# An S5 recurrence step in four vector operations, and the S5 output products in pairs, on one Trainium2 core

## The chip, the cores and the metric

The kernel runs on one core of a Trainium2 chip. The core has five instruction queues that matter here: PE (TensorE, matrix products), DVE (VectorE), ACT (ScalarE), POOL (GpSimd) and SP (SyncE, which only starts transfers). DMA engines move data between main memory and the core. TensorE's weight loads are listed apart from its products, as PEld, because they overlap. The metric is the device time of one execution in microseconds (us); the median of three runs is quoted.

## What is computed

The program is one step of a hybrid trunk of four layers on 384 tokens (128 of a prompt, 256 of a sample) and 1024 channels, all in fp32. Layers 0 and 3 are bidirectional S5 layers, layer 1 is a retention layer, layer 2 a Hyena layer. Each layer normalizes, modulates, mixes, gates and adds. The S5 mixer is what the change touches:

```python
ab_re, ab_im = mag * jnp.cos(lam_im * dt), mag * jnp.sin(lam_im * dt)
...
bu_re = jnp.einsum('blgh,gph->blgp', u, bb_re)
bu_im = jnp.einsum('blgh,gph->blgp', u, bb_im)
...
_, _, h_re, h_im = lax.associative_scan(combine, (a_re, a_im, bu_re, bu_im), axis=1)
y = (jnp.einsum('blgp,ghp->blgh', h_re, c_re.astype(F32))
     - jnp.einsum('blgp,ghp->blgh', h_im, c_im.astype(F32)))
...
y = d_skip.astype(F32) * uf          # then the two directions are added
g = jax.nn.gelu(y)
y = g * jax.nn.sigmoid(g @ w_glu.astype(F32) + b_glu.astype(F32))
```

There are 64 groups of 16 channels. Each group drives a complex diagonal state of 64 numbers, once forward and once backward in time.

## The kernel before

**S5 in chunks.** The 384 tokens are cut into 48 chunks of 8. A chunk's contribution to the state is a product with an expanded table (`use_p`, written P0 to P7 in the plan). The state then steps from chunk to chunk (`recur`, written R0 and R1), and the output of a chunk is a sum of three products: its inputs `U` times a Toeplitz table `Tm` (L880), the forward state times an expanded table `CP` (L881), and the backward state times the other half of `CP` (L882). The 64 groups are 8 blocks `m` of 8 groups. R0 steps the states of blocks 0 to 3 (`X` of half 0), R1 those of blocks 4 to 7.

**The recurrence.** The real and imaginary parts of a state lie 16 partitions apart. One step is five DVE operations on 128x64 elements: a shuffle that swaps the parts (L792), the state times the real table `A[:, 0]` (L793), an addition (L794), the swapped state times the imaginary table `A[:, 1]` (L795), and an addition (L796). Prompt (16 chunks) and sample (32 chunks) are two independent chains, and R0 and R1 are independent too; there are 47 steps for each half and layer.

**The output stage.** The loop at L862 goes over the 8 blocks. Half a block (4 groups) needs one tile of `CP`, 16 of them in all (numbered hb), in 6 buffers. In layer 3 all 16 are loaded from main memory, where they were stored before (`scratch_cpd`, POOL's queue, L867). In layer 0 six of them are loaded (SP's queue) and ten are expanded on the spot: two multiplies on DVE for each half (L628 into `CP`, L629 into a tile `xt` of two buffers), and a DMA from POOL's queue that adds `xt` to `CP` (L631): 20 of each. Blocks 2p and 2p+1 share two PSUM tiles: the even block writes partitions 0 to 63, the odd one 64 to 127. After the odd block the pair is copied out (L889, ACT), transposed (L895) and goes through gelu (L901 to L904, ACT and DVE). `Tm` is transposed by PE (L855) from a loaded `Tt`, three blocks ahead of its use. `tick` after each block issues one background unit; here these are modulation products (L378, L385) for a later layer.

**What sets the order.** A scheduler of the framework sets the order of instructions on each engine when the program is built, from the order written, the buffers and times of its own. Each engine then runs its queue in that order. The plan for layer 3 is `A10 U0 U1 P0 A12 P1 A13 U2 P2 A16 P3 R0 U3 P4 P5 P6 P7 R1`.

**Expansion ahead.** `gen_b1` expands the tables for `use_p` early (`BP`, with a temporary of tag `xt`) and, for six hb of layer 0 and all of layer 3, also `CP`, which it stores (L647). Both expansions take their temporaries from the same ring of three `xt` buffers.

Of the kernel before, what the change touches and what calls it, by code (L numbers as in the profile page):

```python
# [10 lines left out]
F32 = mybir.dt.float32  # L11
# [3 lines left out]
OP = mybir.AluOpType  # L15
# [11 lines left out]
NCH = T // Q  # L27
# [13 lines left out]
CT = 1  # L41
# [2 lines left out]
TO = 2  # L44
BT = 2
BT2 = 0
TMB = 3
CPB = 6
PSG = 3
GK0 = 0  # L50
# [54 lines left out]
def hybrid_trunk(ctx: ExitStack, tc: tile.TileContext, I, O, dbg=None, layers=(0, 1, 2, 3)):  # L105
# [15 lines left out]
    def psm():  # L121
        return pm.tile([128, 512], F32, tag="m", name="psm")
# [414 lines left out]
    def gen_setup(j, pool, fpool, pp, defer=None):  # L537
# [70 lines left out]
        def s_sign():  # L608
            A = A8[j] = cst.tile([128, 2, 128], F32, name=f"A{j}")
            V.tensor_copy(A[:, 0], B1[:, 8])  # L610
            V.tensor_scalar(A[:, 1], BI[:, 8], sgn[:, 0:1], None, op0=OP.mult)
            V.tensor_scalar(FI, FI, sgn[:, 0:1], None, op0=OP.mult)
            V.tensor_scalar(B1, B1, sgn[:, 1:2], None, op0=OP.mult)
            V.tensor_scalar(BI, BI, -1.0, None, op0=OP.mult)
# [9 lines left out]
    def expand(out, rot, T1, T2, x, sl, l0, bufs, eng, add):  # L624
        c1 = T1[:, sl, l0:l0 + 4].rearrange("p e l -> p l e").unsqueeze(3).to_broadcast([128, 4, 8, 16])
        c2 = T2[:, sl, l0:l0 + 4].rearrange("p e l -> p l e").unsqueeze(3).to_broadcast([128, 4, 8, 16])
        t = rot.tile([128, 4, 8, 16], F32, tag="xt", name="xt", bufs=bufs)
        eng.tensor_tensor(out, c1, x[:, 0].unsqueeze(2).to_broadcast([128, 4, 8, 16]), op=OP.mult)  # L628
        eng.tensor_tensor(t, c2, x[:, 1].unsqueeze(2).to_broadcast([128, 4, 8, 16]), op=OP.mult)  # L629
        if add is None:  # L630
            nc.gpsimd.dma_start(out, t, accum_op=OP.add)  # L631
        else:
            add.tensor_tensor(out, out, t, op=OP.add)  # L633

    def expand_c(CP, rot, tb, xc, hb, xb, eng, add):
        for d in range(2):
            expand(CP[:, d], rot, tb["B1"], tb["BI"], xc[:, d], slice(1, 9) if d == 0 else slice(8, 0, -1), d * 64 + hb * 4, xb, eng, add)

    def gen_b1(j, hb, tb, rot, xb=3, nb=1, spill=False):
        if hb % nb == 0:  # L640
            tb["bc"] = rot.tile([128, nb, 2, 2, 2, 4, 16], F32, tag="bc", name="bc", bufs=2)
            (nc.gpsimd if hb > 2 else nc.sync).dma_start(tb["bc"], I["s5bc"][j, hb // 4, :, hb % 4:hb % 4 + nb])
        rb, xc = tb["bc"][:, hb % nb, 0], tb["bc"][:, hb % nb, 1]
        if spill:
            CP = rot.tile([128, 2, 4, 8, 16], F32, tag="CP", name="CP", bufs=1)
            expand_c(CP, rot, tb, xc, hb, xb, V, None)
            getattr(nc, SPQ).dma_start(I["cpd"][hb], CP.rearrange("p d g e c -> p (d g e c)"))  # L647
        S.activation(xc, xc, AF.Copy, scale=tb["sgn"][:, 1:2])
        BPs = []
        for d in range(2):  # L650
            BP = rot.tile([128, 4, 8, 16], F32, tag="BP", name="BP", bufs=max(xb, 2))
            expand(BP, rot, tb["F1"], tb["FI"], rb[:, d], slice(7, None, -1) if d == 0 else slice(0, 8), d * 64 + hb * 4, xb, V, G if j else V)
            BPs.append(BP)
        return BPs, xc
# [43 lines left out]
    def s5(i, j, nxt, begun=lambda: None):  # L698
# [70 lines left out]

        def recur(q):  # L770
            gs = slice(q * XH, (q + 1) * XH)
            A1, A2 = Av[:, 0, :, gs], Av[:, 1, :, gs]
            X, XF = Xs[q], XFs[q]
            Xb = X[:, 0, 0, 0:1]
            V.tensor_copy(XF[:, 0], X[:, 0, CC])
# [67 lines left out]
        Tms = []  # L843

        def toeplitz(m):
            kdm = I["kd"][j * 8 + m]
            Tt = rot.tile([128, 8, 128], F32, tag="Tt", name="Tt")
            for t in range(8):
                src = bass.AP(tensor=kdm.tensor, offset=kdm.offset + (7 - t) * 16, ap=[[1920, 16], [240, 8], [1, 128]])
                nc.sync.dma_start(Tt[16 * t:16 * t + 16], src)  # L850
            Tm = rot.tile([128, 8, 128], F32, tag="Tm", name="Tm", bufs=TMB)
            for r in range(2):
                ps = psm()
                for g in range(4):
                    TE.transpose(ps[:, g * 128:(g + 1) * 128], Tt[:, r * 4 + g, :], ident)  # L855
                S.copy(Tm[:, r * 4:r * 4 + 4, :], ps.rearrange("p (g c) -> p g c", c=128))
            Tms.append(Tm)
        for m in range(TMB):
            toeplitz(m)
        for m in range(8):  # L860
            CP = []
            for r in range(2):  # L862
                c = rot.tile([128, 2, 4, 8, 16], F32, tag="CP", name="CP", bufs=CPB if j == 0 else CP1)
                if j == 0 and 2 * m + r not in SPL:
                    gen_c(j, 2 * m + r, tb, rot, c, 2, V, None)
                else:
                    (CQ if j else nc.sync).dma_start(c.rearrange("p d g e c -> p (d g e c)"), I["cpd"][2 * m + r])  # L867
                CP.append(c)
            Tm = Tms[m]
            hf = m % 2  # L870
            if hf == 0:
                pys = [psm(), psm()]
                Ys = rot.tile([128, 8, 8, 16], F32, tag="Ys", name="Ys", bufs=1)
            for r in range(2):
                for g in range(4):
                    gl = r * 4 + g
                    gg = m * 8 + gl
                    o = pys[r][64 * hf:64 * hf + 64, g * 128:(g + 1) * 128]
                    o48 = pys[r][64 * hf:64 * hf + 48, g * 128:(g + 1) * 128]
# [3 lines left out]
            if m + TMB < 8:  # L883
                toeplitz(m + TMB)
            tick(CT)
            if hf == 0:
                continue
            for r in range(2):
                S.copy(Ys[:, :, r * 4:r * 4 + 4, :], pys[r].rearrange("p (g t i) -> p t g i", g=4, t=8))  # L889
            for hf in range(2):  # L890
                fb = m - 1 + hf
                o = 64 * hf
                pg = psm()
                for t in range(8):
# [682 lines left out]
```

## Time and profile before

| What | Value |
|---|---|
| Runs | 1665.21, 1668.08, 1676.65 us; median 1668.08 us |
| Profiled execution | 1671.79 us, of which 1670.0 us are the span of the profile |
| Granted TensorE clock, mean over the span | 0.946 |
| PE / PEld busy | 1480.2 us (89%) / 1316.1 us (79%) |
| DVE busy | 1254.5 us (75%) |
| ACT busy | 695.5 us (42%) |
| POOL busy | 662.3 us (40%) |

A share is a mean over the whole program. Layer 3's output stage lies at 1528.7 to 1587.4 us of the span; layer 0's ends at about 341 us, and its expansions for it begin at about 222 us. A granted clock of 1.00 is TensorE's upper level (2.4 GHz), 0.50 the lower one (1.2 GHz).

### The profile page before, as it was taken

To read this page: it belongs to the slowest core of one execution; us is meant where nothing else is said; L and a number is where in the kernel's file an instruction comes from. 1 tells how busy PE (TensorE), PEld (TensorE's weight loads), DVE (VectorE), ACT (ScalarE), POOL (GpSimd) and SP (SyncE) were. 2 spreads that over 40 slices of the span, in tenths; PEclk is the share of its full clock that TensorE was granted. 3 is DMA by queue.
4 is the path that set the end of the run, shared out by engine and by line. 5 is a ranking of instruction groups with operands and counts; after the bars stand their busy time and mean duration, and the time that the engine had idled before them with its cause. 6 is when DMAs were issued, how large, how long until landed. Compare 5 with 4: busy or idle time off the path is not lost. (4 is left out here: it accounts for less than half of the span.)

```text
span 1670.0 us, 27794 instructions
## 1 busy us (share of the span) xinstructions
PE 1480.2 (89%) x10370; PEld 1316.1 (79%) x10370; DVE 1254.5 (75%) x3123; ACT 695.5 (42%) x1275; POOL 662.3 (40%) x484
## 2 busy tenths in 40 slices
PE   5777777788789998999979999999999999987996
PEld 3555566577579887889978989989999797776996
DVE  8956996579787777755868988888798864398355
ACT  2535422233333333335355445454454543531343
POOL 2111232215175757551225655655666231231221
PEclk7889898799799999999989999999999999997998
DMA  8588499733655555543333222222322363675431
GB/s 351 171 234 245 130 242 249 213 132 141 219 173 180 185 206 182 190 155 127 126 132 95 93 70 84 99 92 83 98 92 76 134 252 108 198 210 187 114 127 63
DMA packets 107807, 261.41 MB, mean 157 GB/s; under 512 B 28535, under 2 KB 68568, under 8 KB 88088
## 3 DMA queue, kind: packets, MB, share of 16 engines
q1 hardware_dynamic: 80768, 200.12, 36.4%
q0 software_dynamic: 11984, 34.87, 7.6%
q10 hardware_dynamic: 14920, 24.65, 4.1%
q8 instruction: 82, 1.34, 0.3%
q14 instruction: 53, 0.43, 0.1%
HBM read 220.37 MB, written 30.83 MB: 150 GB/s over the span
## 5 line engine op out<-in xcount | busy, mean ns | idle before, releaser
L133 POOL TENSOR_TENSOR wl<-wr,wh 128x1024 fp32r<-128x1024 f32 (+2 forms) x99 | 249.8, 2525 | 309.3 <-ACT wh L161 271.5
L161 ACT CAST wh<-wr 128x1024 fp32r<-128x1024 f32 (+4 forms) x211 | 215.9, 1029 | 293.7 <-PE psd L138 215.0
L138 PE MATMUL psd<-hh,wh 128*128 128x384 f32 x880 | 303.7, 347 | 8.9 <-ACT wh L161 5.0
L138 PE MATMUL psd<-hl,wh 128*128 128x384 f32 x880 | 302.8, 344 | 6.8 <-DVE hl L469 6.3
L138 PE MATMUL psd<-hh,wl 128*128 128x384 f32 x880 | 302.8, 345 | 6.0 <-POOL wl L133 3.5
L148 DVE TENSOR_TENSOR wl<-wr,wh 128x1024 fp32r<-128x1024 f32 (+3 forms) x112 | 146.4, 1309 | 71.4 <-ACT wh L161 70.9
L138 PEld LDWEIGHTS psd<-hh,wh 128*128 128x128 f32 x880 | 167.7, 191 | 20.0 <-ACT wh L161 8.4
L138 PEld LDWEIGHTS psd<-hl,wh 128*128 128x128 f32 x880 | 167.5, 190 | 16.2 <-DVE hl L469 9.1
L138 PEld LDWEIGHTS psd<-hh,wl 128*128 128x128 f32 x880 | 167.1, 190 | 14.6 <-issue 5.9
L138 PE MATMUL psd<-wl,hh 128*128 128x256 f32 x384 | 110.3, 289 | 5.2 <-DVE wl L148 3.8
L138 PE MATMUL psd<-wh,hh 128*128 128x256 f32 x384 | 111.1, 293 | 4.0 <-DVE g L531 2.6
L138 PE MATMUL psd<-wh,hl 128*128 128x256 f32 x384 | 109.1, 286 | 0.0
L378 PE MATMUL psn<-wr,sgc 128*32 128x256 f32 x640 | 58.2, 454 | 49.0 <-DMA wr<-in_mod_w_dram 42.8
L138 PE MATMUL psd<-zb,wh 128*128 128x384 f32 x240 | 80.9, 338 | 0.0
L138 PEld LDWEIGHTS psd<-wl,hh 128*128 128x128 f32 x384 | 74.3, 193 | 6.9 <-DVE wl L148 4.7
L138 PEld LDWEIGHTS psd<-wh,hh 128*128 128x128 f32 x384 | 73.7, 193 | 6.1 <-DVE g L531 3.3
L378 PEld LDWEIGHTS psn<-wr,sgc 128*32 128x32 f32 x640 | 20.1, 122 | 70.6 <-DMA wr<-in_mod_w_dram 44.7
L629 DVE TENSOR_TENSOR xt<-BI,xc 128x512 f32<-128x512 f32 x52 | 45.1, 870 | 40.6 <-POOL CP L633 16.6
L138 PEld LDWEIGHTS psd<-wh,hl 128*128 128x128 f32 x384 | 74.1, 193 | 0.1
L633 POOL TENSOR_TENSOR BP<-BP,xt 128x512 f32<-128x512 f32 x32 | 46.0, 1437 | 65.8 <-DVE xt L629 41.5
L628 DVE TENSOR_TENSOR CP<-B,xc 128x512 f32<-128x512 f32 x52 | 54.3, 1076 | 18.8 <-DMA scratch_cpd_dram<-CP 9.7
L629 DVE TENSOR_TENSOR xt<-FI,bc 128x512 f32<-128x512 f32 x64 | 48.8, 769 | 24.7 <-POOL BP L633 8.9
(388 smaller groups left out, 4015.0 us busy)
## 6 DMA issues: line engine op xcount, KB each, us to landing
wr<-in_mod_w_dram SPq DMA_DIRECT2D x40, 1024.0 KB
wr<-in_hy_w_in_dram SPq DMA_DIRECT2D x32, 1024.0 KB
wr<-in_ret_w_in_dram SPq DMA_DIRECT2D x24, 1024.0 KB
wr<-in_s_w_in_dram SPq DMA_DIRECT2D x16, 1024.0 KB
wm<-in_mod_w_dram SPq DMA_DIRECT2D x8, 1024.0 KB
CP<-xt POOLq DMA_DIRECT2D x32, 256.0 KB, 7.7
Tt<-scratch_kd_dram SPq DMA_DIRECT2D x128, 64.0 KB
wr<-in_s_w_glu_dram SPq DMA_DIRECT2D x8, 1024.0 KB
```

Of the source, the lines that this page charges most:

```text
L133: G.tensor_tensor(out, a, b, op=op)
L138: TE.matmul(out, lhs[a], rhs[b], start=start and i == 0, stop=stop and i == len(combos) - 1)
L148: V.tensor_sub(out, a, b)
L161: S.copy(hi, ap)
L378: TE.matmul(ps[q * 32:(q + 1) * 32, :256], sg[:, kb, 6 - 2 * u:38 - 2 * u], raw[:, kb, :], start=u == 0 and k2 == 0, stop=u == 3 and k2 == 1)
L628: eng.tensor_tensor(out, c1, x[:, 0].unsqueeze(2).to_broadcast([128, 4, 8, 16]), op=OP.mult)
L629: eng.tensor_tensor(t, c2, x[:, 1].unsqueeze(2).to_broadcast([128, 4, 8, 16]), op=OP.mult)
L633: add.tensor_tensor(out, out, t, op=OP.add)
```

## The change

1. A recurrence step is four DVE operations. One multiply of 128x128 takes the state times both tables (`A12`), the shuffle then swaps the parts of the second product, and two additions follow. The sign of `A[:, 1]` is turned accordingly. The temporaries `sw` and `m1` have one buffer each instead of two.
2. The output loop goes over pairs of blocks. For each group of four it issues the product with `Tm` for the even and the odd block, then the two forward ones, then the two backward ones, so that neighbouring products write different PSUM halves. The three products have one line now (L882).
3. `Tm` is kept in halves of 4 groups, 7 buffers of a half instead of 3 of a whole, and is made four blocks ahead. `CP` tiles are asked for in the order 0, 2, 1, 3 | 4, 6, 5, 7 | and so on. The two background units of a pair come after it.
4. In `gen_b1` the expansions that are stored get a tag of their own (`xs`, 2 buffers), those for `BP` one `xt` buffer instead of three; `BP` has three buffers in layer 0 and two in layer 3.

Below, most lines after a changed one move down by one: L880 to L882 become L882, L793/L792/L794/L796 become L793/L794/L795/L796, L378 and L385 become L379 and L386, L895 becomes L894.

```diff
-TMB = 3
+TMB = 4
+TMH = 7
...
-            V.tensor_scalar(A[:, 1], BI[:, 8], sgn[:, 0:1], None, op0=OP.mult)
+            V.tensor_scalar(A[:, 1], BI[:, 8], sgn[:, 1:2], None, op0=OP.mult)
...
-        t = rot.tile([128, 4, 8, 16], F32, tag="xt", name="xt", bufs=bufs)
+        t = rot.tile([128, 4, 8, 16], F32, tag=tag, name="xt", bufs=bufs)
...
-    def gen_b1(j, hb, tb, rot, xb=3, nb=1, spill=False):
+    def gen_b1(j, hb, tb, rot, xb=1, nb=1, spill=False):
...
-            expand_c(CP, rot, tb, xc, hb, xb, V, None)
+            expand_c(CP, rot, tb, xc, hb, 2, V, None, "xs")
...
-            BP = rot.tile([128, 4, 8, 16], F32, tag="BP", name="BP", bufs=max(xb, 2))
+            BP = rot.tile([128, 4, 8, 16], F32, tag="BP", name="BP", bufs=2 if j else 3)
...
-                    sw = tmp.tile([128, 2, XH], F32, tag=f"sw{c0}{q}", name="sw")
-                    m1 = tmp.tile([128, 2, XH], F32, tag=f"m1{c0}{q}", name="m1")
-                    V.stream_shuffle(sw, cur, [(x + 16) % 32 for x in range(32)])
-                    V.tensor_mul(m1, cur, A1)
-                    V.tensor_add(dst, dst, m1)
-                    V.tensor_mul(sw, sw, A2)
+                    sw = tmp.tile([128, 2, XH], F32, tag=f"sw{c0}{q}", name="sw", bufs=1)
+                    m1 = tmp.tile([128, 2, 2, XH], F32, tag=f"m1{c0}{q}", name="m1", bufs=1)
+                    V.tensor_mul(m1, cur.unsqueeze(1).to_broadcast([128, 2, 2, XH]), A12)
+                    V.stream_shuffle(sw, m1[:, 1], [(x + 16) % 32 for x in range(32)])
+                    V.tensor_add(dst, dst, m1[:, 0])
                     V.tensor_add(dst, dst, sw)
...
-            Tm = rot.tile([128, 8, 128], F32, tag="Tm", name="Tm", bufs=TMB)
             for r in range(2):
+                Tm = rot.tile([128, 4, 128], F32, tag="Tm", name="Tm", bufs=TMH)
...
-        for m in range(8):
-            CP = []
-            for r in range(2):
+        for m in range(0, 8, 2):
+            CP = {}
+            for r, mm_ in ((r, m + q) for r in range(2) for q in range(2)):
...
-                    TE.matmul(o, U[:, m, gl * NCH:gl * NCH + 64], Tm[:, gl, :], start=True, stop=False)
-                    TE.matmul(o48, Xs[gg // XH][:, 0, 0:48, gg % XH], CP[r][:, 0, g].rearrange("p a b -> p (a b)"), start=False, stop=False)
-                    TE.matmul(o48, Xs[gg // XH][:, 1, 1:49, gg % XH], CP[r][:, 1, g].rearrange("p a b -> p (a b)"), start=False, stop=True)
...
+                    for k in range(3):
+                        for q in range(2):
+                            gg = (m + q) * 8 + gl
+                            X = Xs[gg // XH]
+                            o = pys[r][64 * q:64 * q + (48 if k else 64), g * 128:(g + 1) * 128]
+                            a, b = ((U[:, m + q, gl * NCH:gl * NCH + 64], Tms[m + q, r][:, g, :]),
+                                    (X[:, 0, 0:48, gg % XH], CP[m + q, r][:, 0, g].rearrange("p a b -> p (a b)")),
+                                    (X[:, 1, 1:49, gg % XH], CP[m + q, r][:, 1, g].rearrange("p a b -> p (a b)")))[k]
+                            TE.matmul(o, a, b, start=k == 0, stop=k == 2)
+            for q in range(2):
+                if m + q + TMB < 8:
+                    toeplitz(m + q + TMB)
+                tick(CT)
```

On PE, at the start of layer 3's output stage, the order before is this (psm is the PSUM tile, X_14480 the state of half 0, U the inputs):

```order
L855 MATMUL psm<-ident,Tt 128x128 x4
L378 MATMUL psn<-wr,sgc 32x256 x24
L881 MATMUL psm<-CP,X_14480 48x128
L882 MATMUL psm<-CP,X_14480 48x128
L880 MATMUL psm<-Tm,U 64x128
L881 MATMUL psm<-CP,X_14480 48x128
L882 MATMUL psm<-CP,X_14480 48x128
L880 MATMUL psm<-Tm,U 64x128
```

At the same place the order of the changed kernel is this; products of the two blocks of a pair now stand next to one another:

```order
L882 MATMUL psm<-Tm,U 64x128
L855 MATMUL psm<-ident,Tt 128x128 x4
L379 MATMUL psn<-wr,sgc 32x256 x8
L882 MATMUL psm<-CP,X_14394 48x128 x4
L882 MATMUL psm<-Tm,U 64x128 x2
L882 MATMUL psm<-CP,X_14394 48x128 x4
L882 MATMUL psm<-Tm,U 64x128 x2
```

Of the 384 output products of both layers, 5 of 364 neighbouring pairs wrote different halves before; now all 367 do.

On DVE, in layer 3, towards the end of R0, three chains run at once (one of X_14480, which is R0, and two of X_14481, which is R1). One round of them before is 15 operations, of which these are the first 11:

```order
L792 STREAM_SHUFFLE sw<-X_14481 128x64
L793 TENSOR_TENSOR m_15528<-X_14481,A_4514 128x64
L792 STREAM_SHUFFLE sw<-X_14480 128x64
L793 TENSOR_TENSOR m_15148<-X_14480,A_4514 128x64
L792 STREAM_SHUFFLE sw<-X_14481 128x64
L793 TENSOR_TENSOR m_15521<-X_14481,A_4514 128x64
L795 TENSOR_TENSOR sw<-sw,A_4514 128x64
L794 TENSOR_TENSOR X_14481<-X_14481,m_15528 128x2x32
L795 TENSOR_TENSOR sw<-sw,A_4514 128x64
L794 TENSOR_TENSOR X_14480<-X_14480,m_15148 128x2x32
L795 TENSOR_TENSOR sw<-sw,A_4514 128x64
```

The round of the changed kernel is 12 operations:

```order
L793 TENSOR_TENSOR m_15053<-X_14394,A_4428 128x128
L793 TENSOR_TENSOR m_15420<-X_14395,A_4428 128x128
L793 TENSOR_TENSOR m_15414<-X_14395,A_4428 128x128
L794 STREAM_SHUFFLE sw<-m_15053 128x64
L795 TENSOR_TENSOR X_14394<-X_14394,m_15053 128x2x32
L794 STREAM_SHUFFLE sw<-m_15420 128x64
L795 TENSOR_TENSOR X_14395<-X_14395,m_15420 128x2x32
L794 STREAM_SHUFFLE sw<-m_15414 128x64
L795 TENSOR_TENSOR X_14395<-X_14395,m_15414 128x2x32
L796 TENSOR_TENSOR X_14394<-X_14394,sw 128x2x32
L796 TENSOR_TENSOR X_14395<-X_14395,sw 128x2x32 x2
```

Before R1 starts, layer 3's DVE queue holds 118 operations of R0 before (23.6 steps) and 103 now (25.75 steps).

On DVE in layer 0, around the last step of R1 (X_201), the queue before ends R1 with 18 of the 20 second multiplies (L629) already ahead of it:

```order
L792 STREAM_SHUFFLE sw<-X_201 128x64
L793 TENSOR_TENSOR m_2566<-X_201,A_399 128x64
L795 TENSOR_TENSOR sw<-sw,A_399 128x64
L794 TENSOR_TENSOR X_201<-X_201,m_2566 128x2x32
L796 TENSOR_TENSOR X_201<-X_201,sw 128x2x32
L629 TENSOR_TENSOR xt<-BI,xc 128x512 x2
L628 TENSOR_TENSOR CP<-B_224,xc 128x512 x2
```

In the changed kernel 13 of them stand ahead of it and 7 behind (L630 is what was L629):

```order
L793 TENSOR_TENSOR m_2473<-X_201,A_399 128x128
L629 TENSOR_TENSOR CP<-B_224,xc 128x512
L794 STREAM_SHUFFLE sw<-m_2473 128x64
L795 TENSOR_TENSOR X_201<-X_201,m_2473 128x2x32
L796 TENSOR_TENSOR X_201<-X_201,sw 128x2x32
L391 TENSOR_TENSOR mod_3027<-psn,vec 128x2x4x2
L395 SCALAR_TENSOR_TENSOR sc_3028<-mod_3027,vec 128x16
L630 TENSOR_TENSOR xt<-BI,xc 128x512 x4
```

Five of the second multiplies, with their transfers, thus moved from ahead of R1's end to behind it.

## Rows read from the trace of the kernel before

**Rows 1.** Busy time in 10 us stretches; the last columns are PE clock, DMA share, GB/s

```profile
1510.00:1520.00 10.00, 6.40 (x61) 5.20 (x59) 10.00 (x83) 0.49 (x1) 0.00 (x0) 1.00 0.75 253
1530.00:1540.00 10.00, 10.00 (x59) 9.36 (x58) 7.71 (x48) 1.07 (x2) 1.10 (x2) 0.59 0.18 56
1540.00:1550.00 10.00, 10.00 (x99) 9.63 (x98) 3.97 (x16) 4.66 (x9) 2.63 (x4) 1.00 0.75 195
...
300.00:310.00 10.00, 1.74 (x7) 1.34 (x8) 6.01 (x15) 1.50 (x3) 3.17 (x4) 0.50 0.76 214
```

**Rows 2.** Chain of waits through layer 3's output stage: start, length, engine, piece

```profile
1528.69 0.67 PE psm L881 x2
1529.36 0.43 PE psm L882 x2
...
1539.16 0.22 PE psm L880 x2
...
1587.42 0.56 PE psd L138 x2
```

**Rows 3.** PE timeline where `use_p` runs: start, length, form, partitions and columns

```profile
1434.05 1.95 PE L746 MATMUL psm<-PB,U 128*64 128x256 f32 x16
1435.93 0.44 PE L138 MATMUL psd<-hh,wh 128*128 128x384 f32 x1
```

**Rows 4.** PE timeline in layer 0, where two blocks' products happen to meet

```profile
331.77 0.27 PE L881 MATMUL psm<-CP,X 128*48 128x128 f32 x1
331.78 0.32 PE L880 MATMUL psm<-Tm,U 128*64 128x128 f32 x1
...
332.16 0.27 PE L881 MATMUL psm<-CP,X 128*48 128x128 f32 x1
332.27 0.38 PE L882 MATMUL psm<-CP,X 128*48 128x128 f32 x2
```

**Rows 5.** DVE timeline in layer 3's recurrence; in brackets what ended idle time

```profile
1472.60 0.18 DVE L775 COPY XF<-X 128x32 f32<-128x32 f32 x1 [0.92 <-ACT X L758]
...
1526.00 0.21 DVE L792 STREAM_SHUFFLE sw<-X 128x64 f32<-128x64 f32 x1
...
1527.35 0.21 DVE L792 STREAM_SHUFFLE sw<-X 128x64 f32<-128x64 f32 x1
...
1529.73 0.23 DVE L792 STREAM_SHUFFLE sw<-X 128x64 f32<-128x64 f32 x1
...
1530.65 0.22 DVE L792 STREAM_SHUFFLE sw<-X 128x64 f32<-128x64 f32 x1
```

**Rows 6.** L793 between R1's start and R0's end: ns min/median/max, first and last start

```profile
L793 DVE TENSOR_TENSOR m<-X,A x58: 201/206/2441, 1473.3 to 1527.8; 128x64 f32<-128x64 f32 x58
```

**Rows 7.** DVE timeline of two 128x128 operations near the program's start

```profile
24.79 0.28 DVE L601 TENSOR_TENSOR B<-B,pa 128x128 f32<-128x128 f32 x1
24.99 0.28 DVE L602 TENSOR_TENSOR BI<-BI,pb 128x128 f32<-128x128 f32 x1
```

**Rows 8.** Layer 0's expansions: the tile CP's accumulating DMAs, and DVE's first and last xt

```profile
L631 POOL DMA_DIRECT2D CP<-xt x20: 839/853/881, 223.3 to 322.2; - x20
...
DMA to landing us min/median/max: 3.3/7.6/11.1
...
222.32 0.68 DVE L629 TENSOR_TENSOR xt<-BI,xc 128x512 f32<-128x512 f32 x1
...
312.24 1.29 DVE L629 TENSOR_TENSOR xt<-BI,xc 128x512 f32<-128x512 f32 x2
```

**Rows 9.** PE timeline and ACT timeline of layer 0: first product of half 1, and the last copy

```profile
312.38 0.61 PE L881 MATMUL psm<-CP,X 128*48 128x128 f32 x2
...
341.48 0.58 ACT L889 COPY Ys<-psm 128x512 f32<-128x512 f32 x1 [6.19 <-PE psm L882]
```

**Rows 10.** DMA issues of layer 3's output stage: count, KB each, median us to landing

```profile
CP<-scratch_cpd_dram POOLq DMA_DIRECT2D x10, 512.0 KB, 4.1
```

**Rows 11.** Waits of DVE in 40 to 166 us: us in total, times, longest

```profile
DVE xt L629 <- DMA CP<-xt: 7.0, 3, 4.6
```

More of the change, by code (lines that the diff above doesn't have):

```diff
@@ L622, in gen_setup, with expand @@
         return dict(B1=B1, BI=BI, F1=F1, FI=FI, sgn=sgn, dsk=dsk, dmask=dmask)
-    def expand(out, rot, T1, T2, x, sl, l0, bufs, eng, add):
+    def expand(out, rot, T1, T2, x, sl, l0, bufs, eng, add, tag="xt"):
         c1 = T1[:, sl, l0:l0 + 4].rearrange("p e l -> p l e").unsqueeze(3).to_broadcast([128, 4, 8, 16])
         c2 = T2[:, sl, l0:l0 + 4].rearrange("p e l -> p l e").unsqueeze(3).to_broadcast([128, 4, 8, 16])
-        t = rot.tile([128, 4, 8, 16], F32, tag="xt", name="xt", bufs=bufs)
+        t = rot.tile([128, 4, 8, 16], F32, tag=tag, name="xt", bufs=bufs)
         eng.tensor_tensor(out, c1, x[:, 0].unsqueeze(2).to_broadcast([128, 4, 8, 16]), op=OP.mult)
@@ L633, in expand, with expand_c @@
             add.tensor_tensor(out, out, t, op=OP.add)
-    def expand_c(CP, rot, tb, xc, hb, xb, eng, add):
+    def expand_c(CP, rot, tb, xc, hb, xb, eng, add, tag="xt"):
         for d in range(2):
-            expand(CP[:, d], rot, tb["B1"], tb["BI"], xc[:, d], slice(1, 9) if d == 0 else slice(8, 0, -1), d * 64 + hb * 4, xb, eng, add)
-    def gen_b1(j, hb, tb, rot, xb=3, nb=1, spill=False):
+            expand(CP[:, d], rot, tb["B1"], tb["BI"], xc[:, d], slice(1, 9) if d == 0 else slice(8, 0, -1), d * 64 + hb * 4, xb, eng, add, tag)
+    def gen_b1(j, hb, tb, rot, xb=1, nb=1, spill=False):
         if hb % nb == 0:
@@ L771, in recur @@
             gs = slice(q * XH, (q + 1) * XH)
-            A1, A2 = Av[:, 0, :, gs], Av[:, 1, :, gs]
+            A12 = Av[:, :, :, gs]
             X, XF = Xs[q], XFs[q]
@@ L842, in s5 @@
         rot = mk(e2, "s5c", 2)
-        Tms = []
+        Tms = {}
         def toeplitz(m):
@@ L855, in toeplitz @@
                     TE.transpose(ps[:, g * 128:(g + 1) * 128], Tt[:, r * 4 + g, :], ident)
-                S.copy(Tm[:, r * 4:r * 4 + 4, :], ps.rearrange("p (g c) -> p g c", c=128))
-            Tms.append(Tm)
+                S.copy(Tm, ps.rearrange("p (g c) -> p g c", c=128))
+                Tms[m, r] = Tm
         for m in range(TMB):
             toeplitz(m)
-        for m in range(8):
-            CP = []
-            for r in range(2):
+        for m in range(0, 8, 2):
+            CP = {}
+            for r, mm_ in ((r, m + q) for r in range(2) for q in range(2)):
                 c = rot.tile([128, 2, 4, 8, 16], F32, tag="CP", name="CP", bufs=CPB if j == 0 else CP1)
-                if j == 0 and 2 * m + r not in SPL:
-                    gen_c(j, 2 * m + r, tb, rot, c, 2, V, None)
-                else:
[L867 to L873, printed above, removed]
+                if j == 0 and 2 * mm_ + r not in SPL:
+                    gen_c(j, 2 * mm_ + r, tb, rot, c, 2, V, None)
+                else:
+                    (CQ if j else nc.sync).dma_start(c.rearrange("p d g e c -> p (d g e c)"), I["cpd"][2 * mm_ + r])
+                CP[mm_, r] = c
+            pys = [psm(), psm()]
+            Ys = rot.tile([128, 8, 8, 16], F32, tag="Ys", name="Ys", bufs=1)
             for r in range(2):
@@ L876, in s5 @@
                     gl = r * 4 + g
-                    gg = m * 8 + gl
-                    o = pys[r][64 * hf:64 * hf + 64, g * 128:(g + 1) * 128]
-                    o48 = pys[r][64 * hf:64 * hf + 48, g * 128:(g + 1) * 128]
-                    TE.matmul(o, U[:, m, gl * NCH:gl * NCH + 64], Tm[:, gl, :], start=True, stop=False)
-                    TE.matmul(o48, Xs[gg // XH][:, 0, 0:48, gg % XH], CP[r][:, 0, g].rearrange("p a b -> p (a b)"), start=False, stop=False)
-                    TE.matmul(o48, Xs[gg // XH][:, 1, 1:49, gg % XH], CP[r][:, 1, g].rearrange("p a b -> p (a b)"), start=False, stop=True)
[L883 to L887, printed above, removed]
+                    for k in range(3):
[11 more added lines that the diff above has]
+                tick(CT)
             for r in range(2):
@@ L890, in s5 @@
             for hf in range(2):
-                fb = m - 1 + hf
+                fb = m + hf
                 o = 64 * hf
```

## The prediction

> **What bounds the kernel now.** I read first the busy time by stretch, to see which engine is full in each stage that the change touches; then the chain of waits, to see what sets the end of a stage; then the timelines, to price single instructions.
>
> In layer 3 two stages follow one another. While the states step, DVE is full and PE is not: 10.00 of 10 us against 6.40 [rows 1]. From 1530 on PE is full, 10.00 of 10, and DVE has 3.97 of 10 [rows 1]. The chain agrees: from 1528.69 to 1587.42 it runs through PE's products, one after another, 0.43 us each at first and 0.22 from 1539 [rows 2]. The reason for the two prices is in the granted clock, 0.59 in 1530 to 1540 and 1.00 after [rows 1], close to the lower and at the upper level (1.2 and 2.4 GHz); PE had been waiting for R0 before that. So in this layer what shortens R0's end counts, and then what shortens PE's 58.7 us.
>
> Layer 0 is another thing. In 300 to 310 PE is busy for 1.74 and DVE for 6.01 of 10 us [rows 1]; neither is full. PE's first product of the second half starts at 312.38, when R1 ends, and the last copy of sums waits until 341.48 for PE [rows 9]. What fills the time is the expansion of the ten `CP` tiles: 20 accumulating DMAs are issued from 223.3 to 322.2, each landing 3.3 to 11.1 us after its issue, and their multiplies are spread from 222.32 to 312.24, 9 pairs of them in 89.9 us, 10.0 us for a pair [rows 8]. R1's steps share the DVE queue with these multiplies, and a multiply that waits for its `xt` buffer holds up all behind it.
>
> **Part 1, the step in four operations.** Operations on 64 elements start 0.1355 us apart when two chains alternate: ten of them lie between 1526.00 and 1527.35 [rows 5], so a step is 5 x 0.1355 = 0.68 us. Operations on 128x128 start 0.20 apart [rows 7]. The new step is 0.20 + 3 x 0.1355 = 0.61, a saving of 0.07. Its bounds are zero, if the wide multiply costs as much as the two it replaces (0.27), and 0.1355, if it costs as little as one of them; the row of two 128x128 operations is the nearest in shape, and I take it. A chain that runs alone waits for itself: 0.92 us a step, from 1529.73 to 1530.65 [rows 5]. There the new step is as long or longer, since the shuffle now waits for the multiply (0.98, estimated as 0.92 plus the 0.07 by which a 128x128 operation starts its successor later). That holds only at ends of chains.
>
> From R1's start at 1472.60, which ACT's copy of the last block gates [rows 5], to R0's end 58 steps are run [rows 6], in an interleaved order: 58 x 0.07 = 4. Before R1 starts, the queue now holds two more steps of R0, done while PE was the slower one, another 1.3. R0 ends 5 us earlier (0 to 9). Some of these multiplies last up to 2.44 us beside the usual 0.2 [rows 6]; I leave that as it is.
>
> The Trainium skill bears on this (VectorE: DVE Perf Modes, "The DRAIN you can't avoid"): an operation there does not start until the pipe of the one before it is empty. By it a step would go from 5 x 0.21 to 0.28 + 3 x 0.21, and the 58 steps would save 8 us. The trace disagrees: the 0.21 us operations start 0.1355 apart [rows 5].
>
> **Part 2, pairs of products in layer 3.** Neighbouring products now write different halves of the partitions. The trace has two places where that happens already. In `use_p` 8 products of 256 columns alternate between the halves and take 1.88 us, 1434.05 to 1435.93, 0.235 each [rows 3]; in one half two times 0.2165 would be due for as many columns, so the ratio is 0.54. In layer 0, where a block of one half happens to run beside one of the other, eight records, which is four products, start between 331.77 and 332.27, 0.125 each [rows 4]. I take 0.12 at the high clock. The bounds are 0.11 (the two fully beside one another) and 0.2165 (no overlap).
>
> The 58.7 us of the stage split as follows. 10.5 us go by at the low clock, 24 products with a group of modulation products. The other 168 products take 168 x 0.2165 = 36.4. What is left, 11.8, is transposes, modulation products and waits. With the change the low clock lasts as long as before, I assume, and in 10.5 us it passes 40 products (0.24 each); 152 remain, 152 x 0.12 = 18.2; the rest is 11.8, and 1 for the second background unit, which now comes at once. Sum 41.5, a gain of 17 (14 to 19).
>
> Two things stand under this cover before and come near the surface after. The `CP` loads, ten of 512 KB with 4.1 us to landing [rows 10], must come in 41 us instead of 59: 5.24 MB were 28.5% of the DMA engines' time and would be 40%. And gelu and the copies of sums on ACT and DVE, 4.66 and 3.97 us in 10 [rows 1], would be 6.6 and 5.6 in 10. Both fit on paper. R1 is no bound: its states are needed by the third pair, half the stage after the start.
>
> **Part 3, layer 0.** The same pairing is worth 96 x 0.1 = 10 us here after R1's end, if products are what the end waits for, and it ends when the last expansion lands. In the new order 13 of the 20 second multiplies stand ahead of R1's last step, where 18 stood; at 10.0 us a pair the 13th comes at 222 + 60 = 282, and R1 ends at about 289, not 312. The expansions go on at their pace: the 20th issue comes at about 318, its landing 7.6 later at 326, and the last products end about 4 us after that. So the end moves from 341 to 330, a gain of 11. If the last landing stays where it was, 322.2 + 7.6 = 330, and eight more for the last pair of blocks, the gain is 3; if fewer stalls of R1 also quicken the multiplies, 16. I take 11, since the order moves five multiplies behind R1.
>
> **Part 4, the temporaries.** With a tag of their own the stored expansions no longer hold up those for `BP`: DVE waited 7.0 us in all for these transfers in the early stage [rows 11]. On the other side `BP` has one `xt` instead of three, so each expansion waits for POOL's or DVE's addition of the one before. Between a gain of 7 and a loss of 3 I take 0, because PE and DMA are both pressed there by the weights. `Tm` in halves and the order of `CP` tiles are counted in parts 2 and 3.
>
> **The sum.** 5 + 17 + 11 = 33. The profiled execution took 1671.8; 1671.8 - 33 = 1638.8. The median of the runs shown is 3.7 lower than that execution, so the forecast is 1635.
>
> **The rivals.** *Layer 0 gives nothing*, because the expansions and their transfers run to the same end whatever PE does. For it speaks that neither PE nor DVE is full there [rows 1]; against it, that R1's end gated PE until 312 [rows 9] and has moved forward in the order. It would give 5 + 17 = 22, so 1646.
>
> *The reload of `CP` takes over in layer 3.* The six buffers come free by pairs of blocks, so that eight loads are wanted in two bursts, on a queue behind POOL's other work. The stage would be about 50 us, midway between 41.5 and 58.7, which loses 8.5 of the gain: 1643, or 1654 if layer 0 gives nothing either. For it speaks the closer supply (40% of the DMA time), against it the 4.1 us to landing [rows 10].
>
> *The pairs do not overlap.* Then part 2 is zero and layer 0 keeps 4 us from R1's earlier end: 5 + 4 = 9, so 1659. The rows on both places speak against it [rows 3, 4]. The Trainium skill (TensorE: Matmul & The Clock Gate, "Part 3: Packing small matmuls — row/col tiling") says that a weight load overlaps products in flight only when their row groups differ, and the two of a pair use the same rows. By that rule the stage would stay at 58.7. The trace bears out the other reading, since in both places the products share all 128 rows as well.
>
> *The low clock stays (slower).* In stretches where PE had gaps the clock was granted at 0.50 [rows 1]. If the shorter products leave PE waiting between pairs, and it stays at 1.2 GHz through the stage, the stage is 10.5 + 2 x (18.2 + 12.8) = 72.5 us, 14 longer than before; with layer 0's gain lost in the same way and the dense products behind both stages begun at the low clock (some 5 us each), the sum is -5 + 14 + 10 = +19: 1687. It costs half of each microsecond that is spent at the low clock beyond the first 10.5, so the kernel is slower than before from about 45 us of it in a stage of 64, layer 0's gain lost. Against it speaks that PE was full through the low stretch, 10.00 of 10, and the clock rose within it [rows 1].
>
> **Chances.** Forecast 0.50; layer 0 gives nothing 0.25; the reload takes over 0.08; no overlap 0.07; the low clock stays 0.04; a larger gain (layer 0 up to 16, early waits gone, R0 earlier by 9) 0.06. A measurement of this kernel can tell a change of about 1% from none, that is 16.7 us: below 1651 is faster, above 1685 slower. Faster takes nearly all of the first two, the larger gain and half of the reload: 0.81. Slower is 0.02 to 0.04, 0.03. The rest, 0.16, is within 1%. The range of 8 in 10 leaves out the cases of no overlap and of the low clock and half of the larger gain: 1619 to 1653.
>
> **What would show it.** In the changed profile the four-operation rounds should start 0.61 us a step apart, and the 128x128 multiply 0.20 before its successor; layer 3's products should run at 0.12 each after some 10 us of low clock, the stage lasting 41 to 43 us between R0's end and the first dense product; in layer 0 R1 should end near 289 and the last copy of sums near 330. The forecast is wrong if in layer 3 PE waits for `CP` or for gelu between the pairs, if the 128x128 multiply costs 0.27, or if PE's last product in layer 0 still waits for a landing at 330 or later.

## The result: 1653.18 us, and where the profile after differs

| | before | changed |
|---|---|---|
| Median of 8 runs each | 1669.07 us | 1653.18 us (1649.24 to 1660.7) |
| Ratio of the changed kernel to that before | | 0.9896, 95% interval [0.9875, 0.9918] |
| Profiled execution / its span | 1671.79 / 1670.0 us | 1654.23 / 1652.1 us |
| Mean granted TensorE clock | 0.946 | 0.942 |

The change makes the kernel 1.0% faster, 17 us by the ratio. The forecast was 1635 us and a gain of 33, so half of it came; 1653.18 lies at the upper end of the range, which is 1653. Two stages of layer 3 carry the account. The product stage, from the first product with R0's states to the first dense product, took 50.5 us where 58.7 stood [rows 2] and 41.5 were forecast. From R1's start to that first product with R0's states it is 50.4 us, 5.7 less than before. In this profile the first dense product comes 18.6 us earlier (1568.8 against 1587.4). The other 4.7 are there when R1 of layer 3 starts (1467.87 against 1472.60 [rows 5]): 3.4 of them already when R0 of layer 0 starts, 1.3 from there on. So 3.4 + 1.3 + 5.7 + 8.2 = 18.6.

Single traces differ in these parts. In the pairs alone and in the run with one ring of xt, which have the same output loop, the stage takes 46.5 and 45.8 us. In two runs whose edits lie in layer 3 alone, R1 of layer 3 starts at 1463.5 and 1477.7. So the 4.7 us ahead of it cannot be put down to the change, and the stage is worth 8 to 13.

**The step.** The DVE timeline of the changed kernel in layer 3, with two chains running and later with one:

```profile
1465.57 0.49 DVE L793 TENSOR_TENSOR m<-X,A 128x128 f32<-128x128 f32 x2
...
1465.98 0.23 DVE L794 STREAM_SHUFFLE sw<-m 128x64 f32<-128x64 f32 x1
1466.11 0.22 DVE L795 TENSOR_TENSOR X<-X,m 128x64 f32<-128x64 f32 x1
...
1466.79 0.49 DVE L793 TENSOR_TENSOR m<-X,A 128x128 f32<-128x128 f32 x2
...
1467.87 0.26 DVE L776 COPY XF<-X 128x32 f32<-128x32 f32 x1
...
1519.38 0.29 DVE L793 TENSOR_TENSOR m<-X,A 128x128 f32<-128x128 f32 x1
...
1520.36 0.29 DVE L793 TENSOR_TENSOR m<-X,A 128x128 f32<-128x128 f32 x1
```

Two steps lie between 1465.57 and 1466.79, 0.61 us a step where 0.68 stood [rows 5]. One chain alone needs 0.98, where it needed 0.92. Both are as forecast. The copy at 1467.87 is R1's start.

**The pairs.** The PE timeline of the changed kernel in layer 3, second pair of blocks:

```profile
1531.09 0.39 PE L882 MATMUL psm<-Tm,U 128*64 128x128 f32 x4
1531.31 0.60 PE L882 MATMUL psm<-CP,X 128*48 128x128 f32 x8
1531.74 0.39 PE L882 MATMUL psm<-Tm,U 128*64 128x128 f32 x4
```

A product is two records, so twelve records are six products. They take 0.65 us, 0.108 each, half of the 0.22 of one half alone [rows 2] and at the lower bound of the forecast. By the Trainium skill (TensorE: Matmul & The Clock Gate, "Part 3: Packing small matmuls — row/col tiling") a weight load overlaps products in flight only when their row groups differ. The trace disagrees: the two products of a pair use the same rows and cost half as much side by side.

**The hole.** Busy time of the changed kernel in layer 3 (columns as in [rows 1]), and below it the chain of waits:

```profile
1510.00:1520.00 10.00, 7.16 (x76) 5.20 (x76) 9.81 (x74) 0.49 (x1) 0.00 (x0) 0.94 0.65 201
...
1530.00:1540.00 10.00, 8.58 (x116) 7.84 (x114) 7.79 (x29) 4.50 (x10) 4.26 (x6) 1.00 1.08 299
1540.00:1550.00 10.00, 2.20 (x10) 1.86 (x11) 0.00 (x0) 1.17 (x2) 0.00 (x0) 0.64 0.80 205
1550.00:1560.00 10.00, 10.00 (x120) 9.48 (x118) 3.89 (x6) 4.45 (x9) 3.07 (x4) 0.68 0.07 14
```

```profile
1518.30 5.84 PE psm L882 x72
...
1528.71 10.38 DMA Tt<-scratch_kd_dram
...
1543.01 6.49 DMA Tt<-scratch_kd_dram
1549.74 1.94 PE psm L855 x8
1551.68 1.48 PE psm L894 x16
1553.16 7.00 PE psm L882 x96
...
1563.37 5.39 PE psm L882 x96
1568.76 0.56 PE psd L139 x2
```

Where PE was full before, it is busy for 2.20 of 10 us in 1540 to 1550. The chain says what it waits for: not for `CP`, not for gelu, but for the tables `Tt` of blocks 6 and 7, which land at 1549. What stands behind that wait in PE's queue is the third pair of blocks, whose own tables were ready. The DMA engines are full while the first of these `Tt` are on their way (share 1.08 in 1530 to 1540, then 0.80). The first 48 products after the hole (96 records) take 7.00 us and the next 48 take 5.39: the granted clock is 0.64 in the hole and 0.68 in the stretch behind it.

The DMA issues of this stage, changed kernel; the `CP` loads land in 9.1 us (median), before in 4.1 [rows 10]:

```profile
CP<-scratch_cpd_dram POOLq DMA_DIRECT2D x10, 512.0 KB, 9.1
```

**Layer 0.** Of the changed kernel, DVE's timeline from R0's start on, PE's, and ACT's last copy:

```profile
161.17 0.18 DVE L776 COPY XF<-X 128x32 f32<-128x32 f32 x1
...
303.67 0.69 DVE L630 TENSOR_TENSOR xt<-BI,xc 128x512 f32<-128x512 f32 x1 [10.84 <-DMA CP<-xt]
...
310.91 0.69 DVE L630 TENSOR_TENSOR xt<-BI,xc 128x512 f32<-128x512 f32 x1 [4.83 <-DMA CP<-xt]
311.51 0.55 DVE L903 SCALAR_TENSOR_TENSOR gf<-gx,psm 128x384 f32<-128x384 f32 x1
```

```profile
312.21 0.70 PE L882 MATMUL psm<-Tm,U 128*64 128x128 f32 x4 [7.34 <-DVE gf L903]
```

```profile
334.05 0.59 ACT L888 COPY Ys<-psm 128x512 f32<-128x512 f32 x1 [7.26 <-PE psm L882]
```

R1 ends at 290.1, and PE's first product of the second half with a state starts at 299.6, 13 us earlier than in [rows 9]. But the last copy comes only 7.4 earlier. R0's start, in the kernel before:

```profile
164.57 0.18 DVE L775 COPY XF<-X 128x32 f32<-128x32 f32 x1 [1.08 <-ACT X L758]
```

So 3.4 of the 7.4 us lie ahead of R0. From R0's start to the last copy it is 172.9 us, before 176.9, and from R0's start to R1 of layer 3 it is 1306.7, before 1308.0. A multiply that waits for its `xt` buffer, that is for an accumulating DMA to land, holds up gelu's L903 behind it on DVE; gelu holds a PSUM tile, and PE waits 7.34 us for it.

### The profile page after: what moved, and what is told of

Read it like the earlier page. It is cut to its first block, busy times and chain, and to the rows that moved or that the text cites. A ratio compares the mean times of both kernels' runs of the same rounds, so it can differ in the third digit from the quotient of the medians.

```text
span 1652.1 us, 27609 instructions
## 1 busy us (share of the span) xinstructions
PE 1460.5 (88%) x10370; PEld 1290.5 (78%) x10370; DVE 1250.0 (76%) x2935; ACT 693.9 (42%) x1275; POOL 663.5 (40%) x484
## 5 line engine op out<-in xcount | busy, mean ns | idle before, releaser
L139 PEld LDWEIGHTS psd<-hh,wh 128*128 128x128 f32 x880 | 168.2, 192 | 26.2 <-issue 14.3
L379 PE MATMUL psn<-wr,sgc 128*32 128x256 f32 x640 | 57.0, 449 | 30.7 <-DMA wr<-in_mod_w_dram 25.5
L630 DVE TENSOR_TENSOR xt<-BI,xc 128x512 f32<-128x512 f32 x52 | 47.2, 911 | 44.9 <-DMA CP<-xt 18.9
L630 DVE TENSOR_TENSOR xt<-FI,bc 128x512 f32<-128x512 f32 x64 | 51.8, 809 | 17.8 <-POOL BP L634 9.8
L632 POOL DMA_DIRECT2D CP<-xt x32 | 28.0, 929 | 92.7 <-DVE xt L630 43.6
L634 POOL TENSOR_TENSOR CP<-CP,xt 128x512 f32<-128x512 f32 x32 | 50.1, 1565 | 31.1 <-DVE xt L630 19.5
```

What stands on the lines that cost most here:

```text
L139: TE.matmul(out, lhs[a], rhs[b], start=start and i == 0, stop=stop and i == len(combos) - 1)
L379: TE.matmul(ps[q * 32:(q + 1) * 32, :256], sg[:, kb, 6 - 2 * u:38 - 2 * u], raw[:, kb, :], start=u == 0 and k2 == 0, stop=u == 3 and k2 == 1)
```

## The experiments

Ratios are to the kernel before. The main theory was that the gain is the sum of the step and the pairs, and that the missing part of layer 3 is the wait for `Tt`. The rivals are named with each run.

**The step alone.** The kernel before with the four-operation step and nothing else:

```diff
-V.stream_shuffle(sw, cur, [(x + 16) % 32 for x in range(32)])
-V.tensor_mul(m1, cur, A1)
-V.tensor_add(dst, dst, m1)
-V.tensor_mul(sw, sw, A2)
+V.tensor_mul(m1, cur.unsqueeze(1).to_broadcast([128, 2, 2, XH]), A12)
+V.stream_shuffle(sw, m1[:, 1], [(x + 16) % 32 for x in range(32)])
+V.tensor_add(dst, dst, m1[:, 0])
 V.tensor_add(dst, dst, sw)
...
```

> The kernel before with the four-operation step alone (products, Tm and expansion buffers as before). Theory (the gain in layer 3 is the sum of an earlier end of R0 and of shorter products): R0 ends some 7 us earlier against the dense products ahead of it, the output stage stays near 58 us, layer 0 changes by less than 4 us; about 1662 us, 7 below the kernel before. Rival (the step is the whole of the gain, and pairing gives nothing): 1653 us, as the whole change.

Measured: 1663.64 us, 0.9961 [0.9942, 0.9979], 6.5 us less. Layer 3's products run from 1522.7 to 1578.9, 56.2 us. From R1's start to the first product with R0's states it is 50.0 us, before 56.1. The rival falls, and the theory holds for layer 3: the step is worth about its own part and no more. It misses in layer 0, where the change was to be under 4 us: the last copy comes at 328.47, 13 us earlier than before (162.6 us from R0's start, before 176.9). Nothing of that is left when R1 of layer 3 starts (1472.7 against 1472.6).

**The pairs alone.** The changed kernel with the old five operations in `recur` (the diff above, the other way).

> The changed kernel with the old five-operation step. Theory: R0 ends as late as before, layer 3's output stage is about 50 us with the same hole before the third pair, layer 0 ends 7 us earlier; about 1658 to 1660 us. Rival (pairing gives nothing): 1669 us. Rival (the step gives nothing): 1653 us.

Measured: 1662.74 us, 0.9939 [0.9916, 0.9961], 10.2 us less. The output stage is 46.5 us long, where 50 were expected, and the hole is in it. That stage (columns as in [rows 1]) and the waits of PE in it:

```profile
1527.40:1573.90 46.50, 37.78 (x481) 35.41 (x481) 23.26 (x95) 17.18 (x34) 11.51 (x16) 0.85 0.56 162
```

```profile
PE psm L856 <- DMA Tt<-scratch_kd_dram: 8.7, 2, 7.0
PE psm L883 <- DVE X L797: 3.4, 1, 3.4
```

The two parts add up: 6.5 + 10.2 = 16.7, the whole change 17.4. Both rivals fall, that of a step worth nothing narrowly: the interval begins at 0.9916, and that of the whole change ends at 0.9918.

**Halves in turn.** The changed kernel with the 24 products of the even block ahead of the 24 of the odd one:

```diff
-for r in range(2):
-    for g in range(4):
-        gl = r * 4 + g
-        for k in range(3):
-            for q in range(2):
+for q in range(2):
+    for r in range(2):
+        for g in range(4):
+            gl = r * 4 + g
+            for k in range(3):
```

> The changed kernel with the products of a pair written one block after the other (24 of the even block, then 24 of the odd one), so that neighbouring products write the same PSUM half; all else as in the change. Theory (neighbours in different halves run beside one another): products start 0.22 us apart instead of 0.11, 5 us more for each of the four pairs of layer 3 where PE is not waiting anyway; layer 3's output stage 58 to 62 us, about 1662 us or more. Rival (the pairs do not overlap; the shorter stage comes from the other order and the earlier tables): 1653 us and 0.11 to be seen nowhere or here too.

Measured: 1668.17 us, 0.9983 [0.9967, 0.9999]. Nearly all of the gain in time is gone. PE's timeline of this run in layer 3:

```profile
1558.03 0.38 PE L882 MATMUL psm<-Tm,U 128*64 128x128 f32 x2
1558.25 0.60 PE L882 MATMUL psm<-CP,X 128*48 128x128 f32 x4
1558.69 0.38 PE L882 MATMUL psm<-Tm,U 128*64 128x128 f32 x2
```

One product (two records) takes 0.22, three take 0.66, so the same instructions in another order take twice as long. The stage is 55.6 us, shorter than the 58 to 62 expected; PE waits for `Tt` only 0.8 us in it. The slower products cover the tables. The step's part is still there in this trace (50.1 us from R1's start to the first product with R0's states); why the time shows less than step and stage together was not taken apart.

**The transposes later.** The changed kernel; the transposes of blocks 6 and 7 are written behind the third pair's products, their loads stay:

```diff
+    return lambda: turn(m, Tt)     # toeplitz: loads now, transposes when called
...
+while late:
+    late.pop(0)()
 for q in range(2):
     if m + q + TMB < 8:
-        toeplitz(m + q + TMB)
+        f = toeplitz(m + q + TMB)
+        if m == 2 and j == 1:
+            late.append(f)
+        else:
+            f()
```

> The changed kernel, but in layer 3 the transposes of the tables of blocks 6 and 7 are written behind the third pair's products instead of ahead of them; their loads stay where they are. Theory (PE stands in its own queue behind transposes whose tables land at 1549 us, while all that the third pair needs is there): the third pair starts at about 1540 instead of 1553, the output stage shrinks from 50 to about 42 us, 1645 us. Rival (the third pair's own CP tiles or states are late, since the DMA engines are full): the hole stays, the wait is put down to CP, 1652 us.

Measured: 1646.79 us, 0.9863 [0.9834, 0.9892], 22.9 us less, 5.5 better than the change, though the two intervals overlap. The stage is 44.6 us. The theory held in direction and not in size: the third pair no longer waits for the tables, and the wait has moved behind it, to the fourth. Waits of PE in that stage:

```profile
PE psm L858 <- DMA Tt<-scratch_kd_dram: 5.4, 1, 5.4
...
PE psm L886 <- DMA CP<-scratch_cpd_dram: 1.4, 1, 1.4
```

**The tables earlier.** The changed kernel with four `Tt` buffers in layer 3, so that the last loads no longer wait for transposes and stand ahead of the GLU's weights in SP's queue:

```diff
-Tt = rot.tile([128, 8, 128], F32, tag="Tt", name="Tt")
+Tt = rot.tile([128, 8, 128], F32, tag="Tt", name="Tt", bufs=4 if j else 2)
```

> The changed kernel with four buffers for the loaded tables Tt in layer 3 instead of two, so that all their loads stand ahead of the weights for the GLU in SP's queue. Theory (the hole is made by the last tables, which are asked for when two Tt buffers come free and then share full DMA engines with 5 MB of CP and 2 MB of weights): no wait for Tt is left, the output stage shrinks from 50 us to 41 to 44, 1645 us, at least as good as the late transposes. Rival (the DMA engines are simply too full, whatever the order; then something else is late, CP or the GLU's weights): 1650 us or more, and the dense products behind the stage wait for their weights.

Measured: 1642.77 us, 0.9835 [0.9798, 0.9872], 27.5 us less, 10 better than the change. Whole stage of the changed kernel, then of this one (columns as in [rows 1]):

```profile
1518.30:1568.80 50.50, 40.15 (x497) 36.97 (x498) 24.15 (x88) 18.73 (x37) 11.50 (x16) 0.83 0.59 176
```

```profile
1514.90:1552.30 37.40, 36.38 (x497) 33.93 (x497) 24.02 (x88) 18.80 (x37) 11.50 (x16) 0.93 0.60 211
```

PE waits 1.0 us for `CP` and not at all for `Tt`; the stage is 37.4 us. The dense products behind it wait 0.9 us for the casts of their weights, so the rival falls: the DMA engines had room for everything, in another order. The granted clock is 0.93 instead of 0.83; with the hole goes a stretch of low clock.

**Half expansions.** Two runs leave out the 20 second multiplies and the 20 accumulating DMAs of layer 0's output stage, so that its ten expanded `CP` tiles hold half a sum: once with pairs and once with the step alone.

```diff
+eng.tensor_tensor(out, c1, x[:, 0].unsqueeze(2).to_broadcast([128, 4, 8, 16]), op=OP.mult)
+if add == "half":
+    return
 t = rot.tile([128, 4, 8, 16], F32, tag=tag, name="xt", bufs=bufs)
-eng.tensor_tensor(out, c1, x[:, 0].unsqueeze(2).to_broadcast([128, 4, 8, 16]), op=OP.mult)
...
-gen_c(j, 2 * mm_ + r, tb, rot, c, 2, V, None)
+gen_c(j, 2 * mm_ + r, tb, rot, c, 2, V, "half")
```

> The changed kernel, but in layer 0's output stage the ten tiles of CP that are expanded on the spot get the first multiply alone: the second multiply and the accumulating DMA are left out (20 of each). Theory (layer 0's end is set by these transfers and by the multiplies that wait for them in DVE's queue): the last copy of sums comes some 25 us earlier than in the changed kernel (near 310 instead of 334), of which a part is given back in layer 1. Rival (R1 and the products set the end): it stays within 5 us.

> The kernel with the four-operation step alone, with the same second multiplies and accumulating DMAs of layer 0's output stage left out. Theory (with the expansions gone, products bound layer 0, and pairing is worth some 10 us there): layer 0's output stage ends 10 us later than in the run with pairs and half expansion. Rival (pairing is worth nothing in layer 0 even then): both end alike.

Measured: 1635.31 us, 0.9781 [0.9745, 0.9816], and 1643.06 us, 0.9841 [0.9805, 0.9877]. The last copy of layer 0, with pairs and then with the step alone:

```profile
297.47 0.58 ACT L890 COPY Ys<-psm 128x512 f32<-128x512 f32 x1 [1.63 <-PE psm L884]
```

```profile
310.29 0.59 ACT L890 COPY Ys<-psm 128x512 f32<-128x512 f32 x1 [0.65 <-PE psm L883]
```

With the expansions the same copy came at 334.05 and 328.47. So multiplies and transfers together do set layer 0's end, by 37 us with pairs and 18 without, and only without them are the pairs worth something there: 12.8 us. Yet when R1 of layer 3 starts, the run with pairs is behind (1451.7 against 1449.8): these 12.8 us are given back on the way. In the run with pairs PE is busy for 3.75 of 10 us in 300 to 310, waiting for the casts of the GLU's weights (3.2 us for ACT, 2.7 for DVE). How the rest is given back was not taken apart.

**One ring of xt again.** The changed kernel with the expansion buffers of before:

```diff
-def gen_b1(j, hb, tb, rot, xb=1, nb=1, spill=False):
+def gen_b1(j, hb, tb, rot, xb=3, nb=1, spill=False):
...
-expand_c(CP, rot, tb, xc, hb, 2, V, None, "xs")
+expand_c(CP, rot, tb, xc, hb, xb, V, None)
...
-BP = rot.tile([128, 4, 8, 16], F32, tag="BP", name="BP", bufs=2 if j else 3)
+BP = rot.tile([128, 4, 8, 16], F32, tag="BP", name="BP", bufs=max(xb, 2))
```

> The changed kernel with one ring of three xt buffers for both kinds of expansion again, and three BP buffers in both layers. Theory (the split gains and costs about as much: it takes away DVE's early waits for the accumulating DMAs, 7 us in all, and makes PE wait for BP at the start of layer 1, where the trace after shows 9.0 us and that before 0.2): 1650 to 1655 us, no wait for BP at 430 to 460. Rival (the split is worth its 7 us): 1659 us.

Measured: 1658.1 us, 0.9908 [0.9879, 0.9937]; the change has 0.9896 [0.9875, 0.9918]. The split is worth nothing that these runs can tell. DVE's early waits of 40 to 166 us, of this run and, below, of the changed kernel:

```profile
DVE xt L630 <- DMA CP<-xt: 9.9, 4, 7.2
```

```profile
DVE xt L630 <- DMA CP<-xt: 2.8, 2, 1.9
```

The split takes most of that wait away (7.0 before [rows 11]), as meant. At the start of layer 1 PE waits for `BP` 9.0 us in the changed kernel, 4.1 here and 0.2 in the kernel before. The expectation that none would be left was wrong: part of that wait comes from elsewhere.

**Three xt buffers.** The run with early tables, and one more `xt` buffer where layer 0 expands on the spot:

```diff
-gen_c(j, 2 * mm_ + r, tb, rot, c, 2, V, None)
+gen_c(j, 2 * mm_ + r, tb, rot, c, 3, V, None)
```

> The run with early tables, and three xt buffers instead of two for the tiles that layer 0 expands in its output stage. Theory (a multiply that waits for its xt buffer, up to 10.8 us in the trace after, holds up gelu behind it on DVE, and PE behind gelu): layer 0's last copy of sums comes 5 to 10 us earlier than with two, half of that is given back in layer 1, 1639 us against 1643. Rival (the transfers themselves are the bound, since the DMA engines are full): the waits turn into waits of PE for the landing, 1643 us.

Measured: 1635.28 us, 0.9783 [0.9753, 0.9814], 36 us less than before, the best version of this study. DVE's wait for `CP<-xt` in layer 0, 18.9 us in the changed kernel and 13.9 with early tables, is down to 1.0; the longest is now the wait for `xc`:

```profile
DVE CP L629 <- DMA xc<-in_s5bc_dram: 10.9, 3, 4.7
...
DVE xt L630 <- DMA CP<-xt: 1.0, 2, 0.8
```

The last copy of layer 0, of this run and, below, with two buffers and early tables:

```profile
324.61 0.59 ACT L888 COPY Ys<-psm 128x512 f32<-128x512 f32 x1 [0.74 <-PE psm L882]
```

```profile
330.47 0.59 ACT L888 COPY Ys<-psm 128x512 f32<-128x512 f32 x1 [7.18 <-PE psm L882]
```

R0 starts at 168.2 and at 162.6, so from there to the last copy it is 156.4 us, against 167.9 with two buffers (167.6 to 173.2 in all full traces with the loop over pairs and two buffers). PE waits 0.6 us for a landing, so the rival (the transfers are the bound) falls; holding up the queue was. In time the gain over early tables, some 8 us, is not clear of the noise: the two intervals overlap.

**Layer 0 block by block.** The run with early tables, with layer 0's old output loop (products, order of `CP`, three tables ahead) and the new one for layer 3 alone:

```diff
+for m in range(0 if j == 0 else 8, 8):
+    ...                                  # the loop of the kernel before
-for m in range(0, 8, 2):
+for m in range(8 if j == 0 else 0, 8, 2):
```

> Layer 3 as in the run with early tables; layer 0's output loop goes block by block again, as before the change (products, order of CP tiles, three tables ahead), with the four-operation step. Theory (with the expansions on the spot a pair needs four CP tiles at once, and that costs layer 0 as much as its shorter products bring: 172.8 us from the start of R0 to the last copy in the trace after, 162.5 in that of the step alone): layer 0 ends some 10 us earlier, and with half of it given back in layer 1 the time is 1638 us. Rival (the difference of the two traces is chance, or is given back wholly): 1643 us or more.

Measured: 1645.47 us, 0.9851 [0.9821, 0.9881], against 0.9835 [0.9798, 0.9872] with pairs in both layers. The theory fell. From R0's start to the last copy it is 166.9 us, with pairs 167.9; the 172.9 of the changed kernel's trace lies within what changes from one trace with pairs to another (167.6 to 173.2). In layer 0 the pairs cost nothing and bring nothing that these runs can tell.

## Why the prediction was half right

The time lies at the upper end of the range, and the mechanism was right in part. By its own chances the prediction gave 0.81 to a time below 1651 and 0.16 to one within 1%; the median of 1653.18 is of the second kind.

1. **The step** (predicted 5 us; measured 5.7 at R0's end, 6.5 in time alone). Right in each term: 0.61 for two chains, 0.98 for one, two more steps of R0 ahead of R1. By the Trainium skill (VectorE: DVE Perf Modes, "The DRAIN you can't avoid") the next operation starts when the pipe is empty, unless it is one that is not held back. The trace shows again that these are not: the 64-element operations of a step start 0.13 apart and last 0.22.

2. **Pairs in layer 3** (predicted 17, between 14 and 19; measured 8.2, in two other traces with the same loop 12.2 and 12.9). The price of a product in a pair was right, 0.108 against 0.12. The step that failed is the sentence that two things come near the surface, `CP` loads and gelu, and that both fit on paper. A third one was not costed: the tables of the last two blocks. They are asked for when `Tt` buffers come free, behind 2 MB of weights on SP's queue, and share the DMA engines with the `CP` loads. Before, the slow products covered that; the halves in turn show the cover, 0.8 us of wait against 8.7 in the pairs alone. Early tables give 37.4 us, better than the 41.5 forecast. So the products were priced soundly, and the loss is this wait with the clock that it takes along. One term was too large: the sum let 40 products go by in 10.5 us at the low clock, but in the changed kernel the first 36 (72 records) take 5.84.

3. **The rival "the reload takes over"** gave 50 us for the stage and a total of 1643 or 1654. Its price was met and its mechanism was not: the DMA engines were crowded, as it said, but what came late were tables, in front of which PE's queue stood. `CP` itself was waited for 0.5 us between the second pair's products. That a time near 1654 came out of it is luck.

4. **Layer 0** (predicted 11; 7.4 at the last copy, 4.0 of it behind R0's start, and 1.3 from there to layer 3's R1). R1's end moved as forecast (290 against 289). The mis-sized term is the time behind it: I let the last expansion be issued at 318 and land at 326; it was issued at 323.1, after multiplies that had waited up to 10.8 us for a buffer, and PE's last products started behind a landing at 331.6. That is the sign which the prediction itself had named for being wrong. The 3 to 16 us held for the last copy and not for what reached layer 3. That layer 0 gives nothing, at 0.25, is nearer to what the runs show: layer 0 block by block and in pairs differ by less than the noise, and the step alone ends layer 0 13 us earlier with nothing left of it at layer 3. What ends earlier in layer 0 can be given back on the way, which no term of the sum had.

5. **The temporaries** (predicted 0, between a gain of 7 and a loss of 3): 0 within the intervals. Both sides are in the traces, less wait for `xt` early and more wait for `BP` later. The 3.4 us ahead of layer 0's R0 are not shown to come from them, since that start lies between 161.2 and 173.5 in traces with the same code ahead of it.

6. **The low clock** did come, and not from the shorter products but from the hole: 0.64 while PE waited, then 7.00 us for the third pair where the fourth took 5.39. With the transposes behind the hole (1.94 us for 8 records and 1.48 for 16, at other places 1.04 and 0.92) that is some 3 us, an estimate from these rows; it did not decide the result.

## What to carry to other kernels

When a stage on PE is to be halved, list every transfer that lands inside it, tables as well as the large operand, with the buffer that its issue waits for and what it stands behind in its queue; a table that slow products covered may be what is late next. A transpose that waits for a load holds up all that stands behind it on PE (8.8 us in the changed kernel), so either its load is issued a stage earlier or it is written behind the work that is ready. Three more buffers, 10 KB a partition in all, were worth some 19 us here, more than the change itself.

## What the runs showed that I had not expected

Products whose results go to different halves of the partitions run at twice the rate even though both read all 128 rows, and the order alone makes the difference: 0.108 us a product alternating, 0.22 in turn. In the changed kernel's trace the same 512 KB loads land in 9.1 us instead of 4.1 (5.2 to 8.6 in the other traces with these pairs and tables), and the small table loads beside them stand in the chain with 10.38 and 6.49 us, while the DMA engines are full for a stretch (1.08) and have room in the stage as a whole (0.59). And the time from the program's start to R0 of layer 0 is 161.2 us in the trace after and 173.5 in that of the late transposes, with the same code ahead of it, so stages of two traces are better compared from a point inside each than from the span's start.
